# Causal masks added on VectorE, a gate's sums one layer later, and modulation rows turned by transposes, in a two-layer attention trunk

## The chip, the cores and the metric

The kernel runs on one NeuronCore of a Trainium2 chip. The core has five engines that run beside each other, each with its own instruction queue: TensorE (PE: matrix products; PEld is its loading of weights), VectorE (DVE), ScalarE (ACT), GpSimd (POOL) and SyncE (SP, which here issues nearly all DMAs). The metric is device time in microseconds (us) for one execution, lower is better. The kernel before takes 326.96 us, the median of three runs (326.69 to 327.68).

## The reference

One sequence of 256 tokens with 1024 features passes two layers. In each, a conditioning vector gives a shift, a scale and a gate (three rows of 1024), the input is normalised and modulated by shift and scale, a mixer runs, and its output times the gate is added to the input:

```
cond = silu(c)
for i in range(2):
    shift, scale, gate = split(cond @ ada_w[i] + ada_b[i], 3)
    h = rms_norm(x, norm_g[i]) * (1 + scale) + shift
    y = nsa_mixer(h, ...) if i == 0 else moba_mixer(h, ...)
    x = x + gate * y
```

The first mixer (NSA) has 16 query heads in 4 groups. Its output is a gated sum of three attentions: over 15 compressed blocks of keys, over selected blocks and over a window. With 256 tokens every valid block is selected and the window reaches back to the start, so the last two are plain causal attentions with keys and values of their own. The compressed one lets token t see a block only when the block's last token is not after t. The second mixer (MoBA) has one block of 256 tokens, so it is plain causal attention too. A masked softmax is `e = exp(s - max(s))`, divided by its sum, with the scores of later keys at minus infinity. Both mixers multiply their attention output by `silu(z)` and by an output matrix.

## The kernel before

Tokens lie on the 128 partitions in two halves (m = 0, 1). Everything is float32 in accuracy: a weight or an activation is split in `parts_of` and `h_parts` into a high part, rounded to the product format fp32r (ScalarE's copy `hi`), and the rest (VectorE's subtraction `lo`), and a product is the sum of three fp32r products, hi by hi, hi by lo and lo by hi. So each weight piece of 512 KB costs one DMA into a `raw` buffer (5 of them), one ScalarE copy, one VectorE subtraction and its products.

The work is in stages: loads, modulation and the first projections of layer 1 (to about 62 us), the rest of its projections (to about 104), its 8 head pairs (`pair_a`) with the second z projection in their gaps, its output product, the update of x and the next normalisation (about 212 to 223), then the same for layer 2, with `z_blocks` beside the 8 calls of `pair_b`, and the output product at the end.

A head pair (2 heads) is a chain across engines. `scores` makes one PSUM tile of scores for two heads by four fp32r products of 256 columns and a fifth in bf16 that adds the causal mask: the identity `identB` is the weight, and a triangle of 0 and -2e38 (`tri`, `tri2`) moves through. `top` takes the negated row maximum with one VectorE reduction over that tile, `exps` is ScalarE's exponential, read from PSUM with the maximum as bias and the row sum as a second output, one instruction per head and block. Then VectorE scales the probabilities, TensorE transposes them (`p_transposed`), ScalarE copies them out and TensorE multiplies by the values. `pair_a` makes three score tiles, `pair_b` two. `compressed` does 8 heads at once, its mask (`maskC`) also by a bf16 product.

The modulation: `ada_rows` multiplies the conditioning vector, held as column 0 of 32 in `condz`, with pieces of ada_w; four tiles of 32 weight columns run in TensorE side by side, so the sums of even and odd pieces lie in rows 0, 32, 64 and 96 of the result. `ada_ss` (shift and scale) turns these rows into columns by products with `selP` (float32, two columns), which also add the even and the odd row. `ada_gate` makes the gate on all partitions. For layer 1 it takes `ada_rows`, a bias row loaded behind it, and float32 products with `selG`. For layer 2 it adds the 8 pieces of ada_w on VectorE, one `scalar_tensor_tensor` over 128x1024 each, and sums over partitions by float32 products with `ones`.

The order of each engine's queue is not that of the program text. Every instruction is recorded by `Plan` and issued by `Plan.issue`, a list scheduler with a cost for each instruction: on each engine it takes what can start first, then the lower level (`URGENT`, `CHAIN`, `FILL`), then the earlier in the text. Weight splitting, products of projections and the gate are `FILL`. All such instructions therefore carry one line, L373, in the profile, and are told apart by their tiles. `side` is a list of generators (compressed keys, the gate of layer 1, shift and scale of layer 2, the gate of layer 2); each call of `beside` lets the first of them emit its next step, so it decides where in the text, and in which order of buffers, their loads and sums stand.

## Time and profile before

| | |
|---|---|
| time, three runs | 326.69, 326.96, 327.68 us |
| span of the profiled execution | 326.3 us |
| PE busy | 314.7 us, 96% |
| DVE busy | 239.7 us, 73% |
| ACT busy | 202.5 us, 62% |
| POOL busy | 26.0 us, 8% |
| moved by DMA | 65.80 MB, 202 GB/s over the span |
| granted TensorE clock | 1.00 |

The span runs from the first to the last instruction of one execution under the hardware profiler. A row of a group of instructions shows the tile written, the tiles read, the shapes, how many there were, their busy time together and the mean duration of one. Matmuls overlap in TensorE's pipeline, so one lasts longer than the distance from its start to the next one's start; that distance is what it costs in a full queue. A row of windows gives, for a stretch of the span, each engine's busy time.

### The profile page before, as it was taken

To read this page: it belongs to the slowest core of one execution; us is meant where nothing else is said; L and a number is where in the kernel's file an instruction comes from. 1 tells how busy PE (TensorE), PEld (TensorE's weight loads), DVE (VectorE), ACT (ScalarE), POOL (GpSimd) and SP (SyncE) were. 2 spreads that over 40 slices of the span, in tenths; PEclk is the share of its full clock that TensorE was granted. 3 is DMA by queue.
4 is the path that set the end of the run, shared out by engine and by line. 5 is a ranking of instruction groups with operands and counts; after the bars stand their busy time and mean duration, and the time that the engine had idled before them with its cause. 6 is when DMAs were issued, how large, how long until landed. Compare 5 with 4: busy or idle time off the path is not lost.

```text
span 326.3 us, 6109 instructions
## 1 busy us (share of the span) xinstructions
PE 314.7 (96%) x2182; PEld 249.0 (76%) x2183; DVE 239.7 (73%) x580; ACT 202.5 (62%) x486; POOL 26.0 (8%) x98
## 2 busy tenths in 40 slices
PE   4899999999999999999999999998999999999995
PEld 4665677777657898679886588866888998988884
DVE  4753375669954999459998665997599899965754
ACT  5635246776536975558776675696675898965420
POOL 7038930000000000000000000000000000000000
PEclk9999999999999999999999999999999999999999
DMA  7999999559898605585267797627376513033102
GB/s 248 307 295 369 367 358 291 172 174 326 274 351 288 231 1 175 213 325 192 66 194 253 233 341 270 203 66 231 91 255 189 157 38 131 0 125 99 38 32 96
DMA packets 43994, 65.80 MB, mean 202 GB/s; under 512 B 4042, under 2 KB 20793, under 8 KB 43964
## 3 DMA queue, kind: packets, MB, share of 16 engines
q1 hardware_dynamic: 43796, 65.36, 60.6%
q8 instruction: 17, 0.28, 0.3%
q14 instruction: 13, 0.11, 0.1%
q10 hardware_dynamic: 168, 0.06, 0.1%
HBM read 64.36 MB, written 1.05 MB: 200 GB/s over the span
## 4 chain that ended last, share of the span: by engine, by line
PE 87%; DMA 4%; DVE 3%; ACT 3%; issue 1%; SPq 0%; ACTq 0%; DVEq 0%
PE ps L373 51%; PE acc L373 36%; DMA early<-in_ada_w_dram 2%; DMA raw<-in_nsa_w_in_dram 2%; ACT hi L373 1%; DVE lo L373 1%; ACT n_in L373 1%; DVE rs L373 1%; DMA rot<-in_c_dram 0%; ACT n_out L373 0%; ACT p L373 0%; DVE HT L373 0%; DVE p L373 0%; DVE y L373 0%; DVE X L373 0%
## 5 line engine op out<-in xcount | busy, mean ns | idle before, releaser
L373 DVE TENSOR_TENSOR lo<-raw,hi 128x1024 fp32r<-128x1024 f32 (+1 forms) x50 | 59.1, 1186 | 26.5 <-ACT hi L373 26.2
L373 ACT CAST hi<-raw 128x1024 fp32r<-128x1024 f32 (+1 forms) x50 | 51.0, 1026 | 32.7 <-PE acc L373 19.5
L373 PE MATMUL acc<-hi,HT 128*128 128x512 f32 (+1 forms) x176 | 54.6, 381 | 1.5 <-ACT HT L373 1.2
L373 PE MATMUL acc<-HT,hi 128*128 128x256 f32 x256 | 50.6, 289 | 0.0
L373 ACT ACTIVATE p<-ps,tiny 128x128 f32<-128x128 f32 (+1 forms) x96 | 39.6, 433 | 9.6 <-DVE tiny L373 9.3
L373 PEld LDWEIGHTS acc<-HT,hi 128*128 128x128 f32 x256 | 40.3, 189 | 0.9 <-issue 0.6
L373 PEld LDWEIGHTS acc<-hi,HT 128*128 128x128 f32 x176 | 32.0, 188 | 10.0 <-issue 2.4
L373 PE MATMUL acc<-HT,lo 128*128 128x256 f32 x128 | 36.9, 289 | 0.0
L373 PE MATMUL acc<-lo,HT 128*128 128x512 f32 (+1 forms) x88 | 33.5, 382 | 0.2 <-DVE lo L373 0.2
L373 PE MATMUL ps<-KTA,qg 128*128 128x256 f32 (+1 forms) x192 | 30.8, 297 | 0.0
L373 PE MATMUL ps<-hi,HT 128*128 128x512 f32 (+1 forms) x96 | 28.2, 367 | 0.0
L373 PEld LDWEIGHTS ps<-KTA,qg 128*128 128x128 f32 x192 | 26.0, 190 | 2.2 <-ACT p L373 1.0
L373 DVE TENSOR_REDUCE tiny<-ps 128x2 f32<-128x512 f32 (+2 forms) x40 | 24.9, 631 | 3.2 <-PE ps L373 2.8
L373 ACT COPY pT<-ps 128x384 f32<-128x384 f32 x48 | 20.9, 488 | 8.6 <-PE ps L373 8.3
L373 PEld LDWEIGHTS acc<-HT,lo 128*128 128x128 f32 x128 | 24.3, 190 | 0.5 <-issue 0.4
L373 PE MATMUL ps<-hi,qg 128*128 128x256 f32 (+1 forms) x96 | 23.6, 320 | 0.0
L373 PE MATMUL acc<-hi,qg 128*128 128x512 f32 x64 | 22.2, 397 | 0.0
L373 ACT ACTIVATION_READ_ACCUMULATOR p<-ps,tiny 128x1 f32 x96 | 20.8, 216 | 0.0
L373 PE MATMUL ps<-identF,p 128*128 128x128 f32 x144 | 20.7, 274 | 0.0
L373 PEld LDWEIGHTS ps<-hi,HT 128*128 128x128 f32 x96 | 16.8, 188 | 4.5 <-issue 2.5
L373 PEld LDWEIGHTS acc<-lo,HT 128*128 128x128 f32 x88 | 16.5, 188 | 3.6 <-DVE lo L373 1.2
L373 PE MATMUL ps<-pT,VA 128*64 128x256 f32 (+1 forms) x192 | 18.9, 334 | 0.0
(203 smaller groups left out, 576.1 us busy)
## 6 DMA issues: line engine op xcount, KB each, us to landing
raw<-in_ada_w_dram SPq DMA_DIRECT2D x32, 512.0 KB, 5.7
raw<-in_moba_w_in_dram SPq DMA_DIRECT2D x20, 512.0 KB, 4.1
early<-in_ada_w_dram SPq DMA_DIRECT2D x12, 512.0 KB, 9.7
raw<-in_nsa_w_in_dram SPq DMA_DIRECT2D x12, 512.0 KB, 6.4
early<-in_nsa_w_in_dram SPq DMA_DIRECT2D x9, 512.0 KB
p<-in_nsa_cmp_w_dram SPq DMA_DIRECT2D x16, 256.0 KB, 4.2
raw<-in_nsa_w_out_dram SPq DMA_DIRECT2D x8, 512.0 KB, 5.7
raw<-in_moba_w_out_dram SPq DMA_DIRECT2D x8, 512.0 KB, 4.2
```

The source lines that it names most:

```text
L373: r = getattr(self.engines[e], method)(*[self._real(a) for a in args], **{k: self._real(a) for k, a in kw.items()})
```

## The change

Masks. `scores` no longer adds the mask. `masked_top` is new: one VectorE instruction per head and block adds a mask from SBUF to the scores in PSUM, negates, writes the result to SBUF and gives its minimum, the negated row maximum, as a second output. `exps` now works on that SBUF copy, with scale -1. `identB`, `tri` and `tri2` go. In `compressed` the mask is added by the VectorE instruction that had copied.

Modulation. `condz` holds the vector in two columns, so every sum of `ada_rows` lies in two neighbouring rows. `ada_ss` turns rows by `transpose` and adds the even and the odd row by a VectorE reduction.

Gates. The sums for both gates are split into hi and lo and multiplied in fp32r. For layer 2 that is two products per half with `onesR`. For layer 1 even rows carry hi and odd rows the rest (`odd` is -1 on odd partitions, else 0), so one product per half does; the bias rows are loaded ahead of the sums and added on the way out of PSUM.

Order. `ada_gate(1)` leaves the first list of `side` and is appended in layer 2, behind its query projections; `z_blocks` of layer 2 and each `pair_b` now call `beside`, and its 8 loads, 8 sums and the rest stand there.

```diff
-    V.tensor_mul(condz[:, :, 0], sg, RT[:, ROW_C:ROW_C + 8])
+    V.tensor_mul(condz[:, :, 0:2], sg[:, :, None].to_broadcast([P, 8, 2]), RT[:, ROW_C:ROW_C + 8][:, :, None].to_broadcast([P, 8, 2]))
...
+        if plus is not None:
+            V.tensor_add(g, acc[:, :n], plus)
+        elif n == P:
...
-                T.matmul(t[:, 2 * q:2 * q + 2], g[:, q * P:(q + 1) * P], selP, start=True, stop=True)
-        tv = t[:, 0:2 * nk].rearrange("p (q s) -> p q s", s=2)
+                T.transpose(t[:, q * P:(q + 1) * P], g[:, q * P:(q + 1) * P], identF)
+        tv = tile_of("ss", nk, 2)
+        V.tensor_reduce(tv, t[:, 0:nk * P].rearrange("p (q s h z) -> p q s h z", q=nk, s=2, h=2)[:, :, :, :, 0],
+                        axis=AX.X, op=OP.add)
...
-            mix, src = (ones, ones), (gate[:, 0:512], gate[:, 512:1024])
+            src = gate
         else:
-            g = yield from ada_rows(l, (2 * D, 2 * D + 512), 512)
+            rows = gate[:, 0:512]
+            G.memset(rows, 0.0)
             for s in range(2):
-                Q.dma_start(g[64 * s + 1:64 * s + 2], bias[:, s * 512:(s + 1) * 512])
-            mix, src = (selG[:, 0], selG[:, 1]), (g, g)
+                for r in (2, 3):
+                    Q.dma_start(rows[64 * s + r:64 * s + r + 1], bias[:, s * 512:(s + 1) * 512])
+            src = yield from ada_rows(l, (2 * D, 2 * D + 512), 512, plus=rows)
+        n = src.shape[1]
+        hi, lo = tile_of("hi", n), tile_of("lo", n)
+        with plan.at(FILL):
+            A.copy(hi, src)
+            if l:
+                V.tensor_sub(lo, src, hi.bitcast(F32))
+            else:
+                V.scalar_tensor_tensor(lo, hi.bitcast(F32), odd, src, op0=OP.mult, op1=OP.add)
         for s in range(2):
             t = tile_of("ps", 512)
...
-                T.matmul(t, mix[s], src[s], start=True, stop=True)
-                A.copy(gate[:, s * 512:(s + 1) * 512], t)
+                with plan.group():
+                    if l:
+                        T.matmul(t, onesR, hi[:, cols], start=True, stop=False)
+                        T.matmul(t, onesR, lo[:, cols], start=False, stop=True)
+                    else:
+                        T.matmul(t, selG[:, s], lo, start=True, stop=True)
+                A.copy(gate[:, cols], t)
...
-            ms = s[:, :, at:at + mk.shape[1]]
-            T.matmul(ms, identB, mk[:, None, :].to_broadcast([P, 2, mk.shape[1]]), start=False, stop=True)
...
-    def exps(dst, src, bias, total):
-        A.activation(dst, src, AF.Exp, bias=bias, accum_out=total)
+    def masked_top(dst, src, neg, at):
+
+        mask = causal[:, P - at:P - at + src.shape[-1]]
+        V.tensor_tensor_reduce(dst, src, mask, -1.0, 3.0e38, op0=OP.add, op1=OP.min, accum_out=neg)
+
+    def exps(dst, bias, total):
+        A.activation(dst, dst, AF.Exp, bias=bias, scale=-1.0, accum_out=total)
...
-    side += [cmp_steps(hid), ada_gate(0), ada_ss(1, 0, 4), ada_gate(1), ada_ss(1, 4, 4)]
+    side += [cmp_steps(hid), ada_gate(0), ada_ss(1, 0, 4), ada_ss(1, 4, 4)]
...
-            T.matmul(s.rearrange("p m h a n -> p (m h a n)"), identB, maskC.rearrange("p m h a n -> p (m h a n)"),
-                     start=True, stop=False)
...
-        V.tensor_copy(pc, s[:, :, :, 1])
+        V.tensor_add(pc, s[:, :, :, 1], maskC[:, :, None, :].to_broadcast([P, 2, 8, 16]))
...
+    side.append(ada_gate(1))
     zT = []
     for c0 in (1536, 2048):
-        at_once(z_blocks(m_in, c0, zT))
+        for _ in z_blocks(m_in, c0, zT):
+            beside()
...
-            s = scores(q, KTB, g, 0, 256, (0, 1), tri, m * P, pm[m])
-            top(neg[:, m], s[:, :, 0:n])
+            s = scores(q, KTB, g, 0, 256, pm[m])
             for e in range(2):
-                exps(pm[m][:, e], s[:, e, 0:n], neg[:, m, e:e + 1], sm[:, m, e:e + 1])
+                masked_top(pm[m][:, e], s[:, e, 0:n], neg[:, m, e:e + 1], m * P)
+            for e in range(2):
+                exps(pm[m][:, e], neg[:, m, e:e + 1], sm[:, m, e:e + 1])
```

In `pair_a` the same is done for its three score tiles: the first gives four `masked_top` of 128 columns, the other two give two each of 256.

## The prediction

> **What bounds the kernel now.** I read the page's busy table first, then the waits of TensorE (PE), then the stages as windows, and last single rows for prices.

> ```profile
> PE 314.7 (96%) x2182; PEld 249.0 (76%) x2183; DVE 239.7 (73%) x580; ACT 202.5 (62%) x486; POOL 26.0 (8%) x98
> PE 87%; DMA 4%; DVE 3%; ACT 3%; issue 1%; SPq 0%; ACTq 0%; DVEq 0%
> ```

> The second line is the chain of work that ended last: 87% of the span is PE following PE. From 100 to 300 us PE waited for others 1.2 us in all:

> ```profile
> PE ps L373 <- DVE n_in L373: 1.0, 1, 1.0
> PE ps L373 <- ACT n_in L373: 0.2, 1, 0.2
> ```

> The stages, with PE, PEld, DVE, ACT and POOL busy in that order, then clock, DMA share and GB/s:

> ```profile
> 12.00:62.00 50.00, 48.55 (x325) 33.71 (x323) 28.00 (x62) 23.82 (x40) 19.91 (x65) 1.00 0.99 323
> 62.00:104.00 42.00, 41.42 (x266) 30.12 (x264) 30.51 (x64) 25.58 (x49) 0.00 (x0) 1.00 0.80 265
> 104.00:191.00 87.00, 86.92 (x704) 68.23 (x705) 70.97 (x198) 60.98 (x199) 0.00 (x0) 1.00 0.58 197
> 191.00:212.00 21.00, 21.00 (x124) 17.91 (x121) 15.69 (x26) 12.33 (x18) 0.00 (x0) 1.00 0.78 265
> 212.00:223.00 11.00, 9.71 (x45) 6.71 (x43) 10.31 (x26) 9.46 (x25) 0.00 (x0) 1.00 0.39 125
> 223.00:245.00 22.00, 22.00 (x102) 17.52 (x101) 16.71 (x34) 15.27 (x27) 0.00 (x0) 1.00 0.57 178
> 245.00:300.00 55.00, 55.00 (x450) 49.66 (x449) 46.02 (x123) 41.67 (x115) 0.00 (x0) 1.00 0.32 104
> 300.00:326.30 26.30, 22.64 (x121) 19.03 (x120) 15.84 (x25) 7.03 (x11) 0.00 (x0) 1.00 0.17 60
> ```

> From 104 us on PE is full in both attention stages (layer 1's head pairs, 104 to 191; layer 2's, 245 to 300), at full clock, with DMA far from full. VectorE is the next engine, at 82% and 84% there. From 12 to 62 us the DMA engines are full too (0.99), so PE time saved there buys nothing.

> **Masks off PE.** A product's price in a full queue is the distance of starts. Around two mask products:

> ```profile
> 150.31 0.39 PE L373 MATMUL ps<-tri,identB 128*128 128x512 bf16 x1
> 150.35 0.82 PE L373 MATMUL ps<-KTA,qg 128*128 128x256 f32 x4
> 151.01 0.28 PE L373 MATMUL ps<-tri,identB 128*128 128x256 bf16 x1
> 151.05 0.37 PE L373 MATMUL acc<-HT,hi 128*128 128x256 f32 x1
> 151.25 0.28 PE L373 MATMUL acc<-HT,lo 128*128 128x256 f32 x1
> 151.37 0.28 PE L373 MATMUL acc<-HT,hi 128*128 128x256 f32 x1
> ```

> From 151.25 to 151.37 one fp32r product of 256 columns costs 0.12. From 151.01 to 151.25 a mask of 256 columns and one such product cost 0.24, so the mask 0.12. From 150.31 to 151.01 a mask of 512 and four products cost 0.70, so that mask 0.70 - 0.48 = 0.22. Per `pair_a` one mask of 512 and two of 256 go, 0.46, eight times 3.7. `compressed` loses two of 512, 0.4. Each `pair_b` loses two of 256, 16 x 0.12 = 1.9. Together **6.0 us**, all on the path.

> **Gates and rows.** Rows of the timeline and one of the chain:

> ```profile
> 178.05 1.02 PE L373 MATMUL ps<-gate,ones 128*128 128x512 f32 x2
> 178.91 0.49 PE L373 MATMUL ps<-identF,p 128*128 128x128 f32 x3
> 187.34 0.95 PE L373 MATMUL ps<-selP,row 128*128 128x2 f32 x8
> 188.15 1.51 PE L373 MATMUL ps<-identF,p 128*128 128x128 f32 x12
> 208.19 2.79 PE acc L373 x12
> L373 PE MATMUL ps<-row,selG 128*128 128x512 f32 x4 | 2.2, 619 | 0.0
> ```

> One float32 product of 512 columns is two records and holds PE from 178.05 to 178.91, 0.86. An fp32r product of 512 costs 2.79 / 12 = 0.23 (output products). Layer 2's gate goes from 2 x 0.86 to 4 x 0.23, saving 0.8. Layer 1's (`selG`, the same shape) goes from 1.72 to 2 x 0.23, saving 1.3. The eight `selP` records of four turned blocks take 187.34 to 188.15, 0.81; four transposes take 4 x 1.51 / 12 = 0.50, so layer 2's two calls save 0.6. Layer 1's five calls lie at 12 to 62 us under full DMA: counted as 0, with bounds of -0.6 (the same saving counts in full) and +1.0 (each call's new VectorE reduction, about 0.2 like the small rows below, delays the first products). **Sum on PE: 6.0 + 0.8 + 1.3 + 0.6 = 8.7 us.**

> **What VectorE gets.** The prices, busy time and mean ns of one:

> ```profile
> L373 DVE TENSOR_REDUCE tiny<-ps 128x2 f32<-128x512 f32 x24 | 16.2, 685 | 1.5 <-PE ps L373 1.3 <-ACT p L373 0.2
> L373 DVE TENSOR_REDUCE tiny<-ps 128x2 f32<-128x256 f32 x8 | 3.4, 419 | 1.0 <-PE ps L373 0.8
> L373 DVE TENSOR_TENSOR y<-ps,gate 128x256 f32<-128x256 f32 x4 | 1.7, 422 | 0.9 <-PE ps L373 0.9
> L373 DVE COPY row<-ps 128x128 f32<-128x128 f32 x2 | 0.6, 292 | 3.1 <-PE ps L373 3.1
> L373 DVE SCALAR_TENSOR_TENSOR gate<-raw,condz,gate 128x1024 f32<-128x1024 f32 x8 | 10.2, 1272 | 0.3 <-DMA raw<-in_ada_w_dram 0.3
> L373 DVE TENSOR_TENSOR lo<-raw,hi 128x1024 fp32r<-128x1024 f32 x46 | 56.0, 1221 | 24.1 <-ACT hi L373 23.8
> L373 DVE TENSOR_SCALAR rs<-ss 128x1 f32<-128x1 f32 x4 | 0.6, 152 | 0.5 <-ACT n_in L373 0.4
> 151.89 0.69 DVE L373 TENSOR_REDUCE tiny<-ps 128x2 f32<-128x512 f32 x1
> 152.49 0.69 DVE L373 TENSOR_TENSOR p<-p,tiny 128x512 f32<-128x512 f32 x1
> ```

> Consecutive VectorE instructions overlap by 0.09 (a reduction of 0.69 at 151.89, the next at 152.49). So a reduction of 512 costs 0.60 and one of 256 0.33. The new `masked_top` stands nowhere in this trace. Its main part is nearest to the two-source read of PSUM with 256 columns (0.42, so 0.33) and, for 128, to the copy from PSUM (0.29, so 0.20). Its second output, the minimum, is bounded below by nothing and above by a small instruction of its own without overlap (0.15). ScalarE's exponentials have such an output, and it shows as a row:

> ```profile
> 151.50 0.39 ACT L373 ACTIVATE p<-ps,tiny 128x128 f32<-128x128 f32 x1
> 151.76 0.22 ACT L373 ACTIVATION_READ_ACCUMULATOR p<-ps,tiny 128x1 f32 x1
> 151.85 0.38 ACT L373 ACTIVATE p<-ps,tiny 128x128 f32<-128x128 f32 x1
> L373 ACT COPY n_in<-ps 128x256 f32<-128x256 f32 x4 | 1.5, 368 | 0.0
> L373 ACT CAST HT<-n_out 128x256 fp32r<-128x256 f32 x8 | 3.2, 404 | 0.2
> ```

> The read of 0.22 begins inside the exponential, and the next exponential starts 0.35 after the last. With the overlap of 0.09 taken from 0.39, the read adds about 0.05. I take 0.06 for VectorE, nearer to this row than to 0.15, because it is the same kind of output, and keep 0 and 0.15 for the range. [...]

> `pair_a`: 4 x 0.20 + 4 x 0.33 + 8 x 0.06 = 2.60 in place of 3 x 0.60, +0.80, eight times **+6.4**. `pair_b`: 2 x 0.20 + 2 x 0.33 + 4 x 0.06 = 1.30 in place of 0.93, +0.37, eight times **+3.0**. In `compressed` a copy becomes an addition of the same size: nothing.

> Layer 1's pairs lose the gate's eight sums, 10.2, and gain 6.4 and some 1.5 for the other gate's bias addition and lo part and for two small reductions: 71.0 - 10.2 + 7.9 = 68.7 us of VectorE work in 87.0 - 7.6 = 79.4 us of PE work. (7.6 is 3.7 + 0.4 + 1.3 + 0.6 and the 1.7 of the second gate's products that leave.) That is 87%, so PE stays the bound and I count no stall.

> Layer 2 is the tight place. Its pairs take 46.0 us of VectorE now. The move brings 10.2 for the sums and 1.2 for the gate's lo part (as the rows of 128x1024), the masks 3.0: 60.4 us. PE there needs 55.0 - 1.9 + 0.9 = 54.0. **VectorE is 6.4 us over** unless work lies elsewhere: the stretch 223 to 245 has 5.3 idle, and 300 to 326 has 10.5. Some of the sums can go ahead into the first, since their loads need only a free buffer, and some splitting of output weights can slip into the second, but the gate is needed at the first update of x, near 305. The bounds of the stall are 0 (all found room) and 6.4 (none did). I take **2.6**, a little under the middle, because most of VectorE's idle time before `lo` is a wait for ScalarE's copy (23.8 of 24.1 us), which the sums do not need.

> **What costs nothing, and its cover.** ScalarE's exponentials now read SBUF; the copies above differ by 0.04 between PSUM and SBUF, 96 x 0.04 = 3.8 us, and the gates add 1.7 of copies. ScalarE has 26.0 us idle in 104 to 191 and 13.3 in 245 to 300; without them it would be 5.5. The order on ScalarE is as before: behind an exponential that waits for its maximum stand the weight copies, and the first exponential of a tile now waits for 0.2 to 0.4 of VectorE, not 0.60. PSUM of a score tile comes free after VectorE rather than after the exponentials, a gain that I don't count. Eight loads of 512 KB move past layer 1's and ahead of some of layer 2's on SP: 245 to 300 moves 55 x 104 GB/s = 5.7 MB, with 4.2 more it is 180 GB/s, under the 323 of the first stage; not hidden, 4.2 MB would cost 13 us. The few constants made at the start (`odd`, `onesR`) are done while PE waits for the first loads.

> **The sum.** Against the span: 326.3 - 8.7 + 2.6 = 320.2. The runs' median stands 326.96 - 326.3 = 0.7 above the span, so the forecast is **320.9 us**.

> **Rivals.** *All of it hides.* VectorE's new work finds room in the 5.3 and 10.5 idle us around the pairs, so the stall is 0: 326.3 - 8.7 + 0.7 = 318.3, and 317.7 with the early rows' 0.6. For it: idle in 223 to 326 is 5.3 + 9.0 + 10.5 = 24.8, more than the 14.4 added. Against: the work has places it must be in.

> *VectorE takes over (slower).* The minimum's read runs as an instruction of its own, 0.15, and nothing overlaps, so `masked_top` costs 0.44 and 0.57. A `pair_b` then takes 2.02 in place of 0.93, +8.7 in all, and the stage 245 to 300 holds 46.0 + 8.7 + 11.4 = 66.1 against 54.0 of PE, 12.1 late. `pair_a` takes 4.04 in place of 1.80, +17.9; layer 1's pairs hold 71.0 - 10.2 + 19.4 = 80.2 against 79.4, 0.8 late. That gives 326.3 - 8.7 + 12.9 + 0.7 = 331.2. It decides once VectorE is more than 8.7 us over PE, which is 16.7 us added in 245 to 300. For it: 84% busy there now. Against: ScalarE's read overlaps.

> *PE's time comes back as gaps.* PE's busy time hides gaps shorter than its pipeline (a product of 0.12 shows 0.28), so a full PE may in fact stand at the pace of the pairs' chains. Then the 8.7 us turn into idle time and the run stays at 327.0. For it: PEld is busy 76%. Against: the rows from 151.01 on follow each other without a gap. [...]

> **Chances.** The forecast with a partial stall 0.48, its own range 318.5 to 324.7 (stall 0.2 to 6.4); all hides 0.22; gaps 0.10; VectorE takes over 0.12; else 0.08. A change under 0.3% (1.0 us) can't be told from none here. Faster takes the first two, half of the rest and a part of the gaps where some gain is left: 0.79; the same 0.08; slower 0.13. The range 316.8 to 326.4 leaves out the takeover and most of the rest.

> **What would show it.** Right: no mask rows; `masked_top` rows near 0.29 and 0.42 with a read that overlaps; PE's busy time near 306; VectorE over 95% in layer 2's pairs, with PE waits there for VectorE's `p` or `lo` of 1 to 6 us; none in layer 1's. Wrong: `masked_top` over 0.5 for 128 columns, PE waits in layer 1's pairs, or a last update of x that waits for the gate.

## The result and the profile after

The changed kernel takes **325.52 us** (median of 20 runs, 323.73 to 326.73) against 326.92 us for the kernel before on the same chip: a ratio of 0.9947, 95% interval 0.9927 to 0.9966. It is faster by 1.4 us where 6.0 were forecast. The profiled execution has a span of 324.7 us, 1.6 less than before.

From the page after: busy time and instructions of each engine, the granted clock of TensorE in 40 slices, and the chain that ended last.

```profile
PE 309.6 (95%) x2123; PEld 245.6 (76%) x2123; DVE 247.0 (76%) x744; ACT 206.7 (64%) x487; POOL 23.9 (7%) x94
PEclk9999999999999997899999999999999999999999
PE 64%; DVE 17%; ACT 8%; DMA 6%; issue 4%; ACTq 0%; DVEq 0%
```

PE is busy 5.1 us less, not 8.7, and the clock row has a dip that the kernel before did not have. TensorE's part of the chain fell from 87% to 64%. Windows of the same trace, with PE, PEld, DVE, ACT, POOL, clock, DMA share and GB/s:

```profile
122.00:125.40 3.40, 2.55 (x22) 1.78 (x15) 3.40 (x17) 2.54 (x12) 0.00 (x0) 0.99 0.47 140
124.00:129.00 5.00, 4.81 (x30) 4.42 (x34) 5.00 (x17) 2.71 (x7) 0.00 (x0) 0.64 0.55 202
129.00:135.00 6.00, 5.85 (x40) 4.20 (x33) 4.50 (x12) 3.71 (x9) 0.00 (x0) 0.73 0.54 176
135.00:185.00 50.00, 49.93 (x421) 40.41 (x420) 37.33 (x159) 38.17 (x123) 0.00 (x0) 1.00 0.59 201
240.00:300.00 60.00, 59.30 (x458) 53.32 (x457) 59.11 (x190) 49.28 (x124) 0.00 (x0) 1.00 0.52 166
```

From 124 to 135 us the granted clock lost 5 x 0.36 + 6 x 0.27 = 3.4 us, that is 6.8 us at half speed (in 127 to 130.5 us it reads 0.50). It falls at 125.36 us and rises at 132.19; in the 3.4 us ahead of the fall PE was busy 2.55 us, 75%. In 240 to 300 VectorE is busy 98.5%, and PE still 98.8%.

Where the time went shows in three stretches, each from a start on PE to a start on PE. Timeline rows of before, then of after: the first scores of layer 1, the first product of layer 2, the last output product.

```profile
103.62 0.64 PE L373 MATMUL ps<-KTA,qg 128*128 128x256 f32 x4
214.98 0.73 PE L373 MATMUL acc<-KTA,HT 128*128 128x512 f32 x2
322.36 0.28 PE L373 MATMUL ps<-hi,qg 128*128 128x256 f32 x1
```

```profile
105.21 1.11 PE L373 MATMUL ps<-KTA,qg 128*128 128x256 f32 x8
212.05 2.98 PE L373 MATMUL acc<-KTA,HT 128*128 128x512 f32 x12
320.93 0.28 PE L373 MATMUL ps<-hi,qg 128*128 128x256 f32 x1
```

| stretch | before | after | forecast | measured |
|---|---|---|---|---|
| to layer 1's first scores | 103.6 | 105.2 | 0 | +1.6 |
| to layer 2's first product | 111.4 | 106.8 | -7.7 | -4.5 |
| to the last output product | 107.4 | 108.9 | +1.6 | +1.5 |

The forecast of the second stretch is layer 1's masks 4.1, the gate products of layer 2 that leave it 1.7, layer 1's gate 1.3 and the rows 0.6. That of the third is 1.9 of masks less, 0.9 of gate products more and the stall of 2.6. So two things are missing: 1.6 us ahead of the pairs, and 3.2 in layer 1's pairs, where the clock lost 3.4.

The stretch in which it fell, PE's timeline of after:

```profile
122.38 0.50 PE L373 MATMUL acc<-HT,hi 128*128 128x256 f32 x2
122.97 0.56 PE L373 MATMUL ps<-identR,n_parts 64*128 64x64 f32 x2
124.19 2.56 PE L373 MATMUL ps<-KTA,qg 128*128 128x32 f32 x16 [0.66 <-ACT KTA L373]
126.59 1.54 PE L373 MATMUL ps<-identF,p 128*128 128x128 f32 x6
127.78 0.81 PE L373 MATMUL ps<-identR,n_parts 128*128 128x128 f32 x4
128.53 1.94 PE L373 MATMUL ps<-raw,condz 128*32 128x512 f32 x8
```

The first `compressed` sends 16 x 32 = 512 columns in 2.4 us (1.9 in the kernel before, at full clock), which one fp32r product sends in 0.23. PE counts as busy all the while, but a tenth of the columns goes through. The clock falls 1.2 us behind the first of them, so the 3.4 us ahead of the fall hold some ten of the 16, the wait of 0.66 us, in which nothing is sent, and the end of a row of `condz` products, which use a quarter of the array (128*32 in their rows, where most others have 128*128). In the kernel before a mask product of 512 columns stood ahead of these 16, and wide z products behind them.

What VectorE got, from the groups of after with shapes kept apart (busy time and mean ns of one), and its timeline around two of them:

```profile
L373 DVE CUSTOM_DVE_ANT_0 p<-ps,causal 128x256 f32<-128x256 f32 x48 | 19.1, 413 | 2.4 <-PE ps L373 2.3 <-ACT p L373 0.2
L373 DVE CUSTOM_DVE_ANT_0 p<-ps,causal 128x128 f32<-128x128 f32 x48 | 12.5, 282 | 0.3 <-PE ps L373 0.2
L373 DVE DVE_READ_ACCUMULATOR2_ANT tiny<- 128x1 f32 x96 | 7.8, 81 | 0.0
```

```profile
109.21 0.42 DVE L373 CUSTOM_DVE_ANT_0 p<-ps,causal 128x256 f32<-128x256 f32 x1
109.56 0.08 DVE L373 DVE_READ_ACCUMULATOR2_ANT tiny<- 128x1 f32 x1
109.56 0.42 DVE L373 TENSOR_TENSOR pcT<-ps,tiny 128x256 f32<-128x256 f32 x1
...
110.74 0.28 DVE L373 CUSTOM_DVE_ANT_0 p<-ps,causal 128x128 f32<-128x128 f32 x1
110.95 0.08 DVE L373 DVE_READ_ACCUMULATOR2_ANT tiny<- 128x1 f32 x1
110.95 0.29 DVE L373 TENSOR_SCALAR g<-g 128x256 f32<-128x256 f32 x1
```

`masked_top` lasts 0.41 and 0.28 us, near the 0.42 and 0.29 of the prediction, and its read of the minimum is a row of its own that starts together with the next instruction, so it costs nothing. From start to start that is 0.35 and 0.21 us.

### The profile page after: what moved, and what is told of

Same layout as the page of the kernel before. It is cut to its first block, busy times and chain, and to the rows that moved or that the text cites. A ratio compares the mean times of both kernels' runs of the same rounds, so it can differ in the third digit from the quotient of the medians.

```text
span 324.7 us, 6133 instructions
## 1 busy us (share of the span) xinstructions
PE 309.6 (95%) x2123; PEld 245.6 (76%) x2123; DVE 247.0 (76%) x744; ACT 206.7 (64%) x487; POOL 23.9 (7%) x94
## 4 chain that ended last, share of the span: by engine, by line
PE 64%; DVE 17%; ACT 8%; DMA 6%; issue 4%; ACTq 0%; DVEq 0%
PE ps L373 41%; PE acc L373 23%; DVE lo L373 4%; DMA raw<-in_nsa_w_in_dram 3%; DVE p L373 3%; DVE rs L373 3%; ACT p L373 2%; DMA early<-in_ada_w_dram 2%; ACT n_out L373 2%; ACT hi L373 1%; DVE n_out L373 1%; DVE gate L373 1%; ACT n_in L373 1%; ACT HT L373 1%; DVE ss L373 1%
## 5 line engine op out<-in xcount | busy, mean ns | idle before, releaser
L373 ACT CAST hi<-raw 128x1024 fp32r<-128x1024 f32 (+1 forms) x50 | 50.7, 1021 | 32.9 <-PE acc L373 17.7
L373 DVE TENSOR_TENSOR lo<-raw,hi 128x1024 fp32r<-128x1024 f32 (+1 forms) x50 | 59.1, 1185 | 16.0 <-ACT hi L373 15.8
L373 PE MATMUL acc<-hi,HT 128*128 128x512 f32 (+1 forms) x176 | 55.1, 384 | 2.6 <-ACT HT L373 1.7
L373 PE MATMUL acc<-HT,hi 128*128 128x256 f32 x256 | 51.5, 288 | 0.7 <-DVE zT L373 0.7
L373 ACT ACTIVATE p<-p,tiny 128x128 f32<-128x128 f32 (+1 forms) x96 | 42.9, 450 | 8.0 <-DVE tiny L373 7.6
L373 PEld LDWEIGHTS acc<-HT,hi 128*128 128x128 f32 x256 | 40.7, 188 | 3.4 <-DVE zT L373 1.7
L373 PEld LDWEIGHTS acc<-hi,HT 128*128 128x128 f32 x176 | 32.0, 188 | 12.0 <-issue 2.4
L373 PE MATMUL acc<-HT,lo 128*128 128x256 f32 x128 | 36.5, 286 | 0.0
L373 PE MATMUL acc<-lo,HT 128*128 128x512 f32 (+1 forms) x88 | 33.6, 384 | 1.4 <-DVE lo L373 1.4
L373 DVE CUSTOM_DVE_ANT_0 p<-ps,causal 128x128 f32<-128x128 f32 (+1 forms) x96 | 31.3, 347 | 2.8 <-PE ps L373 2.5
L373 PE MATMUL ps<-KTA,qg 128*128 128x256 f32 (+1 forms) x192 | 27.9, 288 | 0.8 <-ACT KTA L373 0.7
L373 PE MATMUL ps<-hi,HT 128*128 128x512 f32 (+1 forms) x96 | 28.7, 367 | 0.0
L373 ACT COPY pT<-ps 128x384 f32<-128x384 f32 x48 | 21.6, 482 | 8.2 <-PE ps L373 8.0
L373 PEld LDWEIGHTS ps<-KTA,qg 128*128 128x128 f32 x192 | 24.7, 193 | 1.7 <-ACT KTA L373 0.8
L373 PEld LDWEIGHTS acc<-HT,lo 128*128 128x128 f32 x128 | 24.1, 188 | 0.3 <-issue 0.2
L373 PE MATMUL ps<-hi,qg 128*128 128x256 f32 (+1 forms) x96 | 23.4, 320 | 0.0
L373 PE MATMUL acc<-hi,qg 128*128 128x512 f32 x64 | 22.1, 398 | 0.1
L373 PE MATMUL ps<-identF,p 128*128 128x128 f32 x144 | 21.7, 283 | 0.0
L373 PEld LDWEIGHTS acc<-lo,HT 128*128 128x128 f32 x88 | 16.5, 189 | 5.2 <-DVE lo L373 2.7
L373 PEld LDWEIGHTS ps<-hi,HT 128*128 128x128 f32 x96 | 16.9, 188 | 4.6 <-issue 2.5
L373 PE MATMUL ps<-pT,VA 128*64 128x256 f32 (+1 forms) x192 | 19.1, 334 | 0.0
L373 ACT ACTIVATION_READ_ACCUMULATOR p<-p,tiny 128x1 f32 x96 | 18.2, 190 | 0.0
```

The costliest lines, as they stand in the source:

```text
L373: r = getattr(self.engines[e], method)(*[self._real(a) for a in args], **{k: self._real(a) for k, a in kw.items()})
```

## The experiments

Each run was timed against the kernel before on the same chip; a ratio is to that. "Clock" is the mean granted clock of a run: half speed for 3.4 us, as traced with the masks alone, is about 0.995 of a run, for 6.8 us, as in the changed kernel, 0.989. Of the 100 runs of the kernel before that were timed beside the experiments, 94 were at 0.998 or above and none was below 0.993. In the changed kernel, which was timed twice, 4 of 32 were at 0.998 or above and 14 were at 0.987 to 0.990.

**One part alone.** The kernel before with the masks alone on VectorE:

```diff
-            T.matmul(ms, identB, mk[:, None, :].to_broadcast([P, 2, mk.shape[1]]), start=False, stop=True)
...
+        V.tensor_tensor_reduce(dst, src, mask, -1.0, 3.0e38, op0=OP.add, op1=OP.min, accum_out=neg)
```

> The kernel before, with the masks alone moved to VectorE; the modulation rows, both gates and their places stay as before. Theory A (the PE time saved is real, and three things that the prediction counted at nothing or too low give most of it back: a start of the pairs 1.6 us later that comes with the rows and the gate of layer 1, a drop of the TensorE clock to 0.5 for two 3.413-us periods of about 3.4 us in layer 1's first compressed branch, and VectorE in layer 2): the pairs of layer 1 begin at the old place (first scores near 103.6 us, not 105.2); PE loses 6.0 us of masks; layer 2's pairs without the sums of gate 2 lose nothing to VectorE; with no drop of the clock 320.5 to 322, with one 323 to 325. Theory B (VectorE's added additions alone give the gain back, the clock and the early stage are incidental): 325 to 327, since all of VectorE's added work is here.

Measured: 326.64 us, ratio 0.9973 (0.9944 to 1.0002). First scores at 103.2, the old place, as A had it. The time lies outside A's range and inside B's. The stretch from layer 1's first scores to layer 2, which lost 4.1 of the 6.0 us of masks, grew from 111.4 to 112.8 us. Windows of this run at the end of its pairs:

```profile
185.00:190.00 5.00, 3.57 (x21) 0.92 (x13) 1.59 (x3) 1.95 (x4) 0.00 (x0) 1.00 1.00 339
190.00:195.00 5.00, 5.00 (x26) 4.55 (x26) 3.07 (x6) 3.11 (x3) 0.00 (x0) 0.66 0.99 349
```

and two of its waits in 185 to 215:

```profile
ACT hi L373 <- DMA raw<-in_nsa_w_out_dram: 5.6, 5, 2.3
PE acc L373 <- ACT hi L373: 1.3, 1, 1.3
```

PE stands 1.4 us in 185 to 190 while the DMA engines are full: the pairs end earlier, and the output weights that ScalarE must split are not there yet. The clock falls right behind that, 5 x 0.34 = 1.7 us. The seven runs at a clock of 0.990 to 0.994 took 326.6 to 327.9, three at 0.998 took 324.2 to 324.5, but two at 1.000 took 325.8 and 326.6. The stretch is 5.5 us longer than with 4.1 less: 3.1 of them stand here and 1.0 in PE's waits for ScalarE's `pcT` and `pT`; the rest was not located. In this stretch PE waits nowhere for VectorE, so B's mechanism does not show, though its range holds the time.

At the first `compressed` the mask product is gone in this kernel too, but z products follow its 16 small products (these start at 123.70 us, the z products at 125.79), and the clock stays up:

```profile
123.00:130.00 7.00, 7.00 (x66) 6.96 (x66) 7.00 (x19) 4.67 (x12) 0.00 (x0) 1.00 0.71 234
```

In this execution, then, the mask product's leaving alone brought no drop. In the changed kernel the z products have left the place behind the 16 as well; why the scheduler put them elsewhere was not looked into.

The rest without the masks, the changed kernel with its mask products back on PE:

```diff
+            T.matmul(ms, identB, mk[:, None, :].to_broadcast([P, 2, mk.shape[1]]), start=False, stop=True)
```

> The changed kernel with the bf16 mask products back on TensorE (the compressed branch's mask spread from one copy for its eight heads): only the rows by transposes, the gates and their order are changed. Theory A: no period of the granted clock at 0.5 in layer 1 (mean clock 0.995 or above in every run), PE 2.7 us less than before, 1.6 us lost before the first scores (they begin near 105.2), so 325 to 326.5. Theory B: VectorE has none of the masks, so nothing is given back: 326.9 - 2.7 = 324.2, 323.5 to 324.7.

Measured: 333.43 us, ratio 1.018 (1.0142 to 1.0218); both theories fell. First scores came at 105.8, so the early loss is not the masks'. Layer 2 took 114.3 us in place of 107.4: PE waits of this run behind 220 us, and two windows.

```profile
PE acc L373 <- DVE zT L373: 2.6, 1, 2.6
```

```profile
267.00:272.00 5.00, 2.43 (x20) 2.23 (x20) 5.00 (x14) 4.90 (x20) 0.00 (x0) 1.00 0.31 110
272.00:277.00 5.00, 5.00 (x36) 4.49 (x36) 5.00 (x17) 3.93 (x9) 0.00 (x0) 0.66 0.12 48
```

A z product waits 2.6 us for VectorE, and again half speed follows, 1.7 us. In the changed kernel the same wait is 0.7. So the same place of gate 2's sums goes with a much longer wait than in the changed kernel; that the sums make it was not tried here, nor why it is longer without the masks.

The changed kernel with gate 2 back beside layer 1's pairs:

```diff
-    side += [cmp_steps(hid), ada_gate(0), ada_ss(1, 0, 4), ada_ss(1, 4, 4)]
+    side += [cmp_steps(hid), ada_gate(0), ada_ss(1, 0, 4), ada_gate(1), ada_ss(1, 4, 4)]
...
-    side.append(ada_gate(1))
```

> The changed kernel with the sums of gate 2 back beside layer 1's pairs, where the kernel before has them. Theory A (layer 2's pairs lose some 2 us to a VectorE that is 98.5% busy there, layer 1's have room): layer 2 from its first scores to the end is about 2 us shorter, layer 1's pairs no longer, so 323 to 324.5, the drop of the clock still there in about half of the runs. Theory B (VectorE is the bound in layer 1's pairs too): what layer 2 gains layer 1 loses, 325 to 327.5.

Measured: 329.29 us, ratio 1.0059 (1.0023 to 1.0095): B in direction, beyond its range. PE waits in 145 to 185 us:

```profile
PE acc L373 <- DVE lo L373: 2.0, 1, 2.0
PE ps L373 <- DMA raw<-in_ada_w_dram: 1.3, 1, 1.3
PE ps L373 <- ACT pT L373: 1.1, 2, 0.6
PE ps L373 <- ACT gate L373: 0.7, 1, 0.7
```

With sums and masks in one layer PE waits 5.1 us there, for VectorE's splits, for the gate's loads and for ScalarE. The move of gate 2 is worth some 3.7 us to the changed kernel; A was wrong that layer 1 has room.

**The clock.** Four steps filled the stretch at the first `compressed` with products that are thrown away. Two wide ones ahead of each `compressed`, then four ahead of the first:

```diff
+            for _ in range(2):
+                T.matmul(s.rearrange("p m h a n -> p (m h a n)"), identR, HT[:, 0, 0:2, :].rearrange("p k s -> p (k s)"),
+                         start=True, stop=True)
```

> The changed kernel with two products of 512 fp32r columns that are thrown away ahead of each compressed branch's 16 products of 32 columns (0.23 us each, 0.9 us of PE in all); nothing else is changed and the output is the same. Theory A (the clock drops because the array idles in that stretch): no period at 0.5 in layer 1, mean clock 0.995 or above in most runs; the time is 3.4 us of drop less, where it occurs, and up to 0.9 us more, so 323.8 to 324.8. Theory B (the drop is incidental and the time is VectorE's): the clock as in the changed kernel (0.987 in about half of the runs), 325.5 to 326.4.

> The changed kernel with four products of 512 fp32r columns, thrown away, ahead of the first compressed branch's products alone (none ahead of the second); the output is the same. Theory A (the clock drops where the array streams few columns over one 3.4-us period; a stretch counts as low at a share of the columns streamed under about 0.3, as in the five other profiles): with four products the lowest share there rises from 0.07 to near 0.4, so no run shows a drop in layer 1: mean clock 0.995 or above in all runs, 323.6 to 324.8, the spread of the runs smaller than the changed kernel's 3.0 us. Theory B (the drop has another cause, and two products hit it by luck): mean clock of 0.987 to 0.993 in a third to a half of the runs, median 325.2 to 326.

Measured: 325.33 us, ratio 0.9942 (0.9912 to 0.9973), and 325.58, ratio 0.9947 (0.9917 to 0.9977), no better than the changed kernel. With two, the profiled execution had no drop (span 321.7), and 9 of 12 runs were at 0.995 or above, but the median stayed. With four, 8 of 12 runs were at 0.989 to 0.993: A's numbers fell, and B's fitted. In its trace the drop had moved behind the 16 small products, to some 129 to 132 us (clock 0.88 in 125 to 130 and 0.78 in 130 to 135), where only turned blocks of 128 columns and the quarter-array `condz` products run. Either the drop has another cause, or a fill ahead covers too little. (The shares in the expectations are the columns sent in 3.4 us against what wide products send in that time.)

To make such a stretch in the kernel before: the 16 small products three times, and in another kernel 15 wide ones of the same PE time ahead of them:

```diff
+            for _ in range(0 if hf else 2):
+                for m in range(2):
+                    for h in range(8):
+                        T.matmul(s[:, m, h], QT[g][:, h % 4, m * P:(m + 1) * P], KTA[:, :, g, 512:528],
+                                 start=(m == 0 and h == 0), stop=(m == 1 and h == 7))
```

> The kernel before with the first compressed branch's 16 products of 32 columns done three times (the first two times are thrown away): 32 products more, 0.112 us apart, 3.6 us of a PE that is full by the profile and streams few columns. Theory A (a stretch of few streamed columns, not an idle PE alone, lowers the clock for one or two periods of 3.41 us): the granted clock falls to 0.5 behind it in most runs, mean 0.989 to 0.995, and the time is 3.6 us plus 1.7 to 3.4 us more than before: 332 to 334. Theory B (the drop has to do with a PE that waits, or with VectorE's load): no drop, mean clock 0.998 or above as in the kernel before, 330 to 331.

> The kernel before with 15 products of 512 fp32r columns, thrown away, ahead of the first compressed branch's products: 15 x 0.234 = 3.5 us of PE more in the same place as in the run with more small products. Theory A: no drop, mean clock 0.998 or above, 330 to 331, so 1.7 to 3.4 us less than with the small ones though PE has the same time added. Theory B: the same time as with the small ones, within 0.7 us.

Measured: 343.08 us (ratio 1.0476, 1.044 to 1.0512) and 339.73 (1.0383, 1.0342 to 1.0425). Neither theory had these times: the scheduler put later work elsewhere, and in each of them PE waits 1.4 us for split output weights near 200 us, so the two times do not separate the theories. The clock at the place does. Windows of the run with small products:

```profile
125.00:130.00 5.00, 5.00 (x46) 4.60 (x42) 4.83 (x13) 1.22 (x3) 0.00 (x0) 1.00 0.64 217
130.00:135.00 5.00, 5.00 (x33) 4.87 (x33) 2.66 (x8) 2.23 (x5) 0.00 (x0) 0.56 0.54 206
135.00:140.00 5.00, 5.00 (x26) 3.60 (x26) 0.96 (x4) 1.86 (x4) 0.00 (x0) 0.76 0.00 0
```

and of the run with wide ones:

```profile
130.00:135.00 5.00, 4.83 (x30) 4.05 (x29) 3.32 (x10) 2.55 (x5) 0.00 (x0) 0.66 0.37 139
```

With small products PE is 100% busy, waits for nothing from 125 to 140 us, VectorE is idle half of the time behind 130, and the clock still falls, by 5 x 0.44 + 5 x 0.24 = 3.4 us: for this drop no waiting PE was needed, nor a full VectorE. With wide ones it fell by 1.7 there, though A had expected none: ahead of the small products they don't cover what comes behind.

So the fill was spread over the stretch, three wide products ahead and one behind each four small ones, in the changed kernel alone:

```diff
+            for _ in range(0 if hf else 3):
+                fill(spare)
...
+                    if not hf and (8 * m + h) % 4 == 4 - 1:
+                        fill(spare)
```

> The changed kernel with the seven thrown-away wide products around the first compressed branch alone (three ahead, one after each four of its products); rows by transposes as in the changed kernel, so that nothing but the fill differs. Theory A: every run at a mean clock of 0.995 or above; as the runs of the changed kernel without a drop (324.0) plus 0.9 us of products that no wait covers: 324 to 325, some 1 us less than the changed kernel's 325.5 at the median and with a spread under 2.5 us. Rival (the fill took the drop away only together with the rows by products, whose earlier start shifts the stretch against the clock's periods): 0.987 to 0.989 in a third or more of the runs, 325.5 to 326.

Measured: **324.27 us**, ratio 0.9899 (0.9864 to 0.9934). All six runs were at 0.999 or 1.000, where 14 of 32 of the changed kernel, timed apart from them, were at 0.990 or below. Its window over the stretch:

```profile
124.00:131.00 7.00, 6.98 (x51) 5.62 (x47) 7.00 (x28) 5.67 (x19) 0.00 (x0) 1.00 0.43 151
```

With 1.6 us of useless products the median is 1.3 us lower (the intervals of the two ratios just overlap). The clock stays up in all six runs with the fill (0.999 or 1.000), and narrow products added to the kernel before bring a drop (0.56 in 130 to 135 us) at a PE that is full: in these runs the drop goes with few columns sent in the stretch. The fill also covers PE's wait of 0.66 us, in which no columns are sent; how much of the drop is that wait's and how much the narrow products' was not separated. Unfilled, the drop comes in a part of the executions only, so the median shows a part of the 3.4 us.

**The early loss.** Rows turned by float32 products again in all seven calls; gate 1's bias rows loaded behind its products:

```diff
-                T.transpose(t[:, q * P:(q + 1) * P], g[:, q * P:(q + 1) * P], identF)
+                T.matmul(t[:, 2 * q:2 * q + 2], g[:, q * P:(q + 1) * P], selP, start=True, stop=True)
```

```diff
+                        with plan.group(after=(last,)):
+                            Q.dma_start(rows[64 * s + r:64 * s + r + 1], bias[:, s * 512:(s + 1) * 512])
```

> The changed kernel with the modulation rows turned by float32 products with two columns again, in all seven calls (the selecting columns hold 0.5, since each sum stands in two rows now). Theory A1 (the 1.0 to 1.5 us lost before layer 1's pairs come with the transposes, the added reduction and the waits behind it): first scores back at 103.2 to 103.6, and the time 1 to 1.5 us less than the changed kernel's, less some 0.6 us of PE for the two calls of layer 2's rows: 324.4 to 325.2. Theory A2 (they come with gate 1's four bias rows, which SP issues ahead of the weights): first scores still at 104.3 to 105.8, the time as the changed kernel's or 0.6 us above it: 325.5 to 326.2.

> The changed kernel with the four bias rows of gate 1 loaded behind its last product, not ahead of the weights of the gate on SP's queue. Theory A1 (the early loss comes with the transposed rows): first scores still at 104.3 to 105.8, time 325 to 326. Theory A2 (the early loss comes with the four bias rows on SP): first scores at 103.2 to 103.8, time 1 to 1.5 us less: 324 to 324.6. Either way the order of the steps beside layer 1's pairs is another one, which may move the drop of the clock.

Measured: 325.38 us, ratio 0.9931 (0.9901 to 0.9961), and 325.25, ratio 0.9911 (0.9876 to 0.9946); first scores at 104.2 and 104.5. The late bias rows came out as A1 had it; with the rows by products the time fits neither range. The starts do not decide it, the PE waits from 10 to 105 us do. The changed kernel:

```profile
PE acc L373 <- ACT HT L373: 1.7, 2, 1.0
PE acc L373 <- ACT n_in L373: 0.9, 1, 0.9
PE ps L373 <- DVE p L373: 0.6, 1, 0.6
```

Rows by products:

```profile
PE acc L373 <- ACT HT L373: 1.3, 2, 1.1
PE acc L373 <- ACT n_in L373: 1.3, 1, 1.3
PE ps L373 <- DVE p L373: 0.3, 1, 0.3
```

The waits at 30.8 (`HT`) and 64.9 us (`p`) go from 0.79 and 0.63 to 0.27 and 0.28, as in the kernel before, 0.87 together; with the late bias rows they stayed at 0.78 and 0.62. They belong to the transposed rows of layer 1. The third, at 80 us, is a weight copy that stands ahead of `n_in` on ScalarE. It was 0.3 in the kernel before, 0.8 with the masks alone and 0.4 to 1.3 elsewhere: what decides it was not found. So layer 1's five calls by products, layer 2's two by transposes, run on two chips, the second time beside the changed kernel itself:

```diff
+                if l:
+                    T.transpose(t[:, q * P:(q + 1) * P], g[:, q * P:(q + 1) * P], identF)
+                else:
+                    T.matmul(t[:, 2 * q:2 * q + 2], g[:, q * P:(q + 1) * P], selP, start=True, stop=True)
```

> The changed kernel with float32 products (columns of 0.5) for layer 1's five calls of modulation rows, which stand on the way to the first products, and transposes for layer 2's two calls, which lie beside the pairs. Theory A1 (the transposed rows cost 0.85 us early, in the waits at 30.8 and 64.9 us, and save 0.6 us beside the pairs): those two waits at 0.27 and 0.29 us again, and 0.85 us less than the changed kernel: 324.4 to 325. Rival (the waits only move to the next late link, as the wait at 80 us did when all rows were turned by products): 325.2 to 325.8.

> The changed kernel itself, unchanged, beside the two below on one chip: 325.5, with a mean clock of 0.987 to 0.989 in about half of its runs and 0.995 or above in a third.

> Products for layer 1's rows and transposes for layer 2's, once more beside the changed kernel: Theory A: 0.85 us less than the changed kernel in the runs of like clock. Rival (the first comparison was chance): within 0.3 us of it.

Measured: 324.68 us, ratio 0.9896 (0.9847 to 0.9945); on the second chip 323.69, ratio 0.9890 (0.9861 to 0.9919), beside 325.65 and 0.9943 (0.9913 to 0.9972) for the changed kernel. (323.69 is the median of five executions; the sixth, the profiled one, took 747.21 us and is left out.) The two waits were 0.27 and 0.28 us in the first of these profiles. The medians gain 0.8 and 2.0 us; on the second chip the executions at a clock of 0.993 to 0.995 take 323.6 us on average against 324.8 for the changed kernel, 1.1 less, near the 0.85 of A. The intervals of the two kernels overlap, so the size is not settled.

**Layer 2.** Gate 2's sums cut to 8 of 1024 columns (the rest of that gate is left out):

```diff
-                    V.scalar_tensor_tensor(gate, w, condz[:, kk, 0:1], gate, op0=OP.mult, op1=OP.add)
+                    V.scalar_tensor_tensor(gate[:, 0:8], w[:, 0:8], condz[:, kk, 0:1], gate[:, 0:8], op0=OP.mult, op1=OP.add)
```

> The changed kernel with gate 2's sums on VectorE cut to the first 8 of 1024 columns (the rest of gate 2 is left out; its loads, its split and its products stay): some 8 x 1.1 us less of VectorE in layer 2. Theory A (layer 2 loses the 2.6 us that the prediction took for a full VectorE): from the first product of layer 2 to its last output product 2 to 2.6 us less than the 108.9 us of the changed kernel, so 323 to 323.6, with the drop in layer 1 as it was. Theory C (VectorE at 98.5% in layer 2 holds nothing up, and what layer 2 loses comes from the transition between the layers and the tail): 0 to 0.7 us less, 324.8 to 325.5.

Measured: 324.98 us, ratio 0.9923 (0.9893 to 0.9953). Layer 2, from the first product at 210.3 to the last at 317.9, took 107.6 us, 1.3 less than in the changed kernel: between A and C. PE's wait for `zT` of 0.7 was gone. The other 1.2 of the 2.5 that layer 2 loses does not come from the sums. 0.9 of it stands at the start of layer 2, PE's waits of the changed kernel in 212 to 230 us:

```profile
PE acc L373 <- DVE lo L373: 1.2, 2, 0.6
PE ps L373 <- DVE n_in L373: 0.4, 1, 0.4
PE acc L373 <- ACT VA L373: 0.3, 1, 0.3
```

That is 1.9 us, mostly for weight splits, against 1.0 in the kernel before (of its 1.2 us in the prediction, 0.2 lies ahead of the first product of layer 2). With the sums cut these waits stay. The last 0.3 was not located.

Could GpSimd take the sums?

```diff
-                    V.scalar_tensor_tensor(gate, w, condz[:, kk, 0:1], gate, op0=OP.mult, op1=OP.add)
+                    G.tensor_scalar_mul(w, w, condz[:, kk, 0:1])
+                    G.tensor_add(gate, gate, w)
```

> The run before (products for layer 1's rows, transposes for layer 2's) with gate 2's sums on GpSimd, which has nothing to do after the setup, in two steps each (weights times the condition in place, then an addition): VectorE has 8.8 us less in layer 2. Theory A (a full VectorE costs layer 2 the 1.3 us that went when the sums were cut to 8 columns): 1.3 us less than the run before, 323 to 324; GpSimd is done before the gate is read near 295 us. Rival (GpSimd is slow, over 5 us a load, and the weight buffers that its sums hold are late for the products of layer 2): 327 or more.

Measured: 344.12 us, ratio 1.0494 (1.045 to 1.0538): the rival's time, though not its way. GpSimd's groups in 240 to 290 us, and VectorE's in 241 to 286 of this run:

```profile
L373 POOL TENSOR_SCALAR raw<-raw,condz 128x1024 f32<-128x1024 f32 x8 | 25.5, 3190 | 195.4 <-DVE lo L373 193.8 <-DVE rs L373 1.6
L373 POOL TENSOR_TENSOR gate<-gate,raw 128x1024 f32<-128x1024 f32 x8 | 20.0, 2498 | 0.6
```

```profile
L373 DVE SCALAR_TENSOR_TENSOR rs<-rs 128x16 f32<-128x16 f32 x6 | 6.7, 1114 | 0.1
L373 DVE TENSOR_TENSOR n_out<-n_out,rot 128x256 f32<-128x256 f32 x2 | 3.0, 1495 | 0.0
```

GpSimd needs 5.7 us a piece, and VectorE gets slower beside it (below). PE waited 8.2 us at once for VectorE, up to 264 us, and not for weight buffers as the rival had it.

**Both repairs together**, products for layer 1's rows and the spread fill:

> The same kernel with seven products of 512 fp32r columns, thrown away, around the first compressed branch: three ahead, then one after each four of its 16 products of 32 columns: 7 x 0.23 = 1.6 us of PE, of which some 0.67 us falls into the wait ahead of the branch. Theory A (few streamed columns over one period make the drop): the lowest share there rises from 0.12 to about 0.4, no run shows 0.987 to 0.989, the median clock is 0.995 or above; 0.9 us more than the undropped runs of the kernel without it (322.5), so 323 to 324, with a spread under 2 us. Theory B (the drop has another cause): half of the runs at 0.987 to 0.992, and 325.5 to 326.

Measured: **323.30 us** (322.37 to 324.73), ratio 0.9886 (0.9858 to 0.9914), the lowest median of all. All six runs were at 0.998 or above. Beside the same kernel without the fill on the same chip, 323.69, the gain is 0.4 us and the intervals overlap, so what the fill adds to the time here is not shown; of the five runs without it one was at 0.987 and one above 0.995. Less the 7 x 0.23 = 1.6 us of thrown-away products, PE's busy time is near the 306 that was forecast:

```profile
PE 307.5 (96%) x2138; PEld 245.0 (76%) x2138; DVE 246.4 (77%) x739; ACT 207.0 (64%) x487; POOL 25.3 (8%) x97
```

## Why the prediction was wrong

**PE's saving was real.** Busy PE fell by 5.1 us in a trace that holds 3.4 us lost to the clock: 8.5 against the 8.7 of the sum. Together the masks, the gates and the rows were priced right. The rest of the span is idle PE: 326.3 - 314.7 = 11.6 us before and 324.7 - 309.6 = 15.1 after, 3.5 more, and -8.5 + 3.4 + 3.5 is the 1.6 by which the span fell. The sum had 2.6 for idle PE, all in layer 2's pairs, and nothing for the clock.

**The step that failed: the clock.** The sum took PE's prices at full clock and had no term for what is left when wide products leave from around narrow ones: here the mask product ahead of the 16 of the first `compressed` and the z products behind them. That is 3.4 us in the profiled execution. At the median the kernel with the fill is 1.3 us faster, with its own 1.6 us of thrown-away products in that time. The windows of before showed clock 1.00 throughout, and the prediction read that as a property of the stage. No rival had this either: "PE time comes back as gaps" said 327.0 by gaps spread over the pairs; the 3.5 us of idle PE that did come stand at a few waits that the profile names, and from 135 to 185 us PE shows none.

**The second step: "counted as 0".** Layer 1's five calls of rows have the bound of +1.0 in the prediction. Their two waits measured +0.87; some half a microsecond more came from a wait on ScalarE whose cause is open. The prediction argued that PE time saved under full DMA buys nothing, and no run contradicts that, but delay is not covered by that: the calls stand on the chain to the first products.

**Layer 2's stall came out at the forecast size, 2.5 us against 2.6, by luck:** it is made of two parts, 1.3 for the sums and 1.2 for other things, mainly at the start of the layer, where the sum had no stall. VectorE's share of 98.5% was foreseen, and full VectorE cost PE little: the sign named for it, 1 to 6 us of PE waits in the pairs, came as 0.7. The masks gave VectorE less than priced: at 0.21 and 0.35 us from start to start, `pair_a` adds 0.44 and not 0.80, `pair_b` 0.19 and not 0.37.

**The rivals.** "VectorE takes over" needed 0.44 and 0.57; the rows refute it for this kernel. But with gate 2's sums left in layer 1 a part of it happens there: at 329.29 us, 2.0 of the 5.1 us of PE's waits are for VectorE. "All of it hides" fails by the same two terms as the forecast. Nor did all of PE's saving come back as gaps, with PEld busy 76% before and after: the execution without a drop, with two wide products ahead of each `compressed`, took 323.6 us, 3.6 less than the 327.2 of the kernel before on its chip.

**The parts do not add up.** By their ratios the masks alone gained 0.9 us (not clear of none), the rest alone lost 5.9, and together they gained 1.7. What the traces show beside it: with the masks alone the output weights were late, with the rest alone the z products, with both neither was late by more than 0.7 us. That it is the removal of gate 2's eight loads from layer 1 which lets the output weights come in time was argued, not tried.

## What to carry to other kernels

When a full TensorE loses wide products, look at what is left around the narrow ones: here 16 products of 32 columns, all of them busy time, stood where the clock fell to 0.50 for 6.8 us, and with 1.6 us of useless wide products spread among them it stayed at 0.999 or above and the median was 1.3 us lower. A wait of TensorE may cost twice, once itself and once by the clock behind it: 1.4 us with the masks alone and 2.6 with the rest alone were each followed by a loss of 1.7, though with gate 2 back in layer 1 a wait of 2.0 us was followed by none. Cost a change on the chain ahead of a full engine as delay, whatever the engine saves, and before adding up parts ask which transfer or engine is late next when one part goes in alone.

## What the runs showed of the hardware that was not expected

Some VectorE instructions beside a running GpSimd took several times as long: the six small `rs` of the rows above 1.11 us in the mean (one 2.37, another 0.17), and 0.18 in the same place without GpSimd; the two additions on 256 columns 1.50 in the mean against 0.43. The twelve `rs` of another kind (plain two-input) stayed at 0.17. Which instructions are hit was not looked into.

VectorE's second output is an instruction of its own (96 reads, 0.08 us each). It cost no time, since the next instruction starts with it (both at 109.56 us in the timeline above). So the 0.06 that the prediction took for each, from ScalarE's row, was not needed here.
